# Moving three pieces of DVE work, and a group of transposes, in the output stage of a hybrid decoder layer

## The chip, the cores and the metric

The kernel runs on one core of a Trainium2 chip. The metric is the device time of one execution in microseconds (us). Several engines run their own instruction streams side by side and wait for each other by semaphores: TensorE (PE: matrix products and transposes), VectorE (DVE), ScalarE (ACT), GpSimd (POOL) and the DMA queues (SP issues most of them).

## What is computed

One layer of a decoder over 4096 prompt tokens and 64 sample tokens, model width 1024. The tokens are normalised and projected by `w_in`; three groups of heads (a gated convolution, sliding-window attention over 128 keys, and cross-attention into 256 memory tokens) give a row of 1024 values per token; `w_out` projects that back, and the result is normalised and added to the input.

```python
h = _rmsnorm(x, g_pre)
z = h @ w_in
cb, cc, ch, cg, q, k, v, ag, mq, mg = _split_cols(z)
...
out_a = jax.nn.silu(cg) * cb * conv                                  # convolution
out_b = jax.nn.silu(ag) * o_b        # o_b: window attention with sinks, 8 heads
out_c = jax.nn.silu(mg) * o_c        # o_c: attention into the memory tokens, 4 heads
y = jnp.concatenate([out_a, out_b, out_c], axis=-1) @ w_out
return x + _rmsnorm(y, g_post), new_conv, new_k, new_v
```

## The kernel before

**Stages.** The input projection comes first and lasts until about 918 us. Then attention and output projection run interleaved until the end. The prompt is cut into 16 chunks of 256 tokens; the two halves of a chunk have 128 tokens each and are numbered h = 0 to 31 (an even h is the first half of its chunk).

**Output projection.** The first six blocks of 128 tokens (blocks 0 to 5, `Block.run`) multiply `mix` (the 1024 values per token) with the eight 128-row slices of `w_out`, for each column half p and slice k. Every factor is split into a rounded part ("hi") and the remainder ("low"), so one slice is three products. From chunk 3 on two blocks are one `Pair` (c = 3 to 15, `Pair.run`): for the upper half of the inner dimension it uses Strassen-like sums, so that fewer products are needed. A pair has four accumulators, c12, c21, c11 and c22, and operands made ahead by POOL (the sum), ACT (the cast, "hi") and DVE (the subtraction, "low"): `pa` plain parts, `pr` row sums, `pw0` and `pw1` window parts, `pd` the diagonal sum, `pc` column differences. `lows` makes the two parts of any of them (L1676 the cast, L1679 the subtraction). `added` (L1755 for the second block) is the last addition of a pair: it reads the accumulator c22. L1772, L1775 and L1778 are the additions between c12, c21 and c11. L1761 and L1751 multiply with the norm's weights, L1740 squares and sums, L1746 copies an accumulator out.

**Finishing a block.** A finished block leaves a function in the list `left`: `finish` (L1658) multiplies by the norm's factor, adds the input `xr` in place and issues the store `o_yp<-xr`. `finish_block` empties that list.

**Attention.** For each half: window scores (`ws`, L1331), their masks and softmax on DVE and ACT (L1341, L1279, L1287, L1295 the division that gives `sm`), transposes of `sm_0` and `sm_1` on PE (`wt`, L1376), copies on ACT (`wpt`, L1305), selections on POOL that split the band (`wpv`, L1310, and `wpt`, L1313), and the products with the values (`wo`, L1388 and L1394). The cross-attention scores (`xs`) go through a maximum (L1169), exponentials on ACT (`xp`, L1178), a reciprocal (`xrd`, L1184), a scaling on POOL (L1190), transposes (`xt`, L1366), one ACT copy back to `xp` (L1367), and products (L1059).

**Order.** PE's order is written by hand in one manual schedule, until pair 13 begins; from there on it is left to the scheduler, up to the end of the last pair. The order counts in steps, "an eighth" in the words of the change: one step is one slice's three products. A block has 16 steps, a pair 30. `at(n, fn)` hangs a piece of work on step n; `first_at`, `memory_at` and `second_at` say at which step the scores, the cross-attention scores and the transposes of each half are issued. The other engines' orders follow a list scheduler, except for what `keep_in_program_order` pins. `between` is an existing list of work left for a later moment.

```python
turn_of = lambda odd, even: {h: start_of((h - 3) // 2) + (odd if h % 2 else even) for h in range(9, 2 * NCH + 1)}
second_at = {h: n + (12 if h == 2 else 9 if h == 8 else 8) for h, n in first_at.items()} | turn_of(18, 32)
...
at(e - 3, p.row_sums)
at(e + 4, lambda p=p: p.window_parts(0))
at(e + 7, lambda p=p: p.window_parts(1))
```

Here e is the first step of pair c, so `row_sums` of pair c is issued three steps before the end of pair c - 1.

**Weights of the pairs.** While blocks 0 to 5 run, the sums of `w_out` slices for the pairs (`wtT`, `wsumT`: L1842, L1847, L1848) are made on DVE and ACT, two of them are parked in memory, and they are loaded over slices of `wo` just before pair 3 (`wo<-tdT`).

Of the kernel before, what the change touches and what calls it, by code (L numbers as in the profile page):

```python
# [12 lines left out]
ALU = mybir.AluOpType  # L13
AX = mybir.AxisListType

P = 128
# [11 lines left out]
NCH = 4096 // CT  # L28
# [19 lines left out]
def f(ap):  # L48
    return ap.bitcast(F32)
# [3 lines left out]
def hybrid_layer(ctx: ExitStack, tc: tile.TileContext, a: dict):  # L53
# [1525 lines left out]
    class Block:  # L1579
# [38 lines left out]
        def run(self, starts):  # L1618
            b, m = self.b, self.m
            yn = work([P, D], "yn", f"yn{b}")  # L1620
            dst = a["o_ys"] if b == 32 else a["o_yp"][b * P : (b + 1) * P, :]
            st = tiny.tile([P, 4], F32, tag="ms", name=f"yst{b}")

            for p in range(2):
                cs = slice(512 * p, 512 * p + 512)
                acc = psum("z", f"y{b}_{p}")
                for k in range(KT):
                    starts.get((p, k), lambda: None)()
                    if m < P:
                        l, w = self.terms[p][k]  # L1630
                        for r in range(2):
                            TE.matmul(acc, l, w[:, r], start=k + r == 0, stop=k + r == KT)
                        continue
                    if (p, k) == (0, 5):
                        finish_block()
                    for i, (l, r) in enumerate(((0, 0), (1, 0), (0, 1))):
                        TE.matmul(acc, self.hl[l][:, k], wo[k][p][:, r], start=k + i == 0, stop=k + i == KT + 1)  # L1637
                if m < P:
                    S.copy(yn[:m, cs], acc[m : 2 * m])
                    V.tensor_tensor(yn[:m, cs], acc[:m], yn[:m, cs], op=ALU.add)  # L1640
                    junk = sums["sum"].tile([P, 512], F32, tag="sum", name=f"junk_s{p}")
                    S.activation(junk[:m], yn[:m, cs], AF.Square, scale=float(D) ** -0.5, accum_out=st[:m, p : p + 1])
                    V.tensor_tensor(yn[:m, cs], yn[:m, cs], gpost[:m, cs], op=ALU.mult)
                    continue
                V.tensor_tensor(yn[:m, cs], acc[:m], gpost[:m, cs], op=ALU.mult)
                S.activation(acc[:m], acc[:m], AF.Square, scale=float(D) ** -0.5, accum_out=st[:m, p : p + 1])  # L1646
            self.factor(st)
            left.append(lambda queued, part=None: self.finish(yn, st, dst, queued, part=part))
# [14 lines left out]
    class Pair:  # L1663
# [24 lines left out]
        def sums_of(self, raw, t, *terms):  # L1688
# [4 lines left out]
                G.tensor_tensor(raw[:, n * i : n * i + n], x, y, op=op)  # L1693
            return lambda pinned=False: self.lows(t, raw, pinned)

        def row_sums(self):
            t = self.parts("pr")
            self.rows = [t[:, :, 0:2], t[:, :, 2:4]]
            raw = sums["sum"].tile([P, 512], F32, tag="sum", name=f"sum{self.c}")
            self.sums_of(raw, t, *((self.mix(slice(2, 4), n), self.mix(slice(0, 2), n), ALU.add) for n in range(2)))()  # L1700

        def window_parts(self, n):
            t = self.w[n] = self.parts(f"pw{n}_")
# [17 lines left out]
        def run(self, starts, sample=lambda: None):  # L1721
            c, last = self.c, self.c == NCH - 1
# [30 lines left out]
            def added(n, p, acc):  # L1753
                cs = (left_, right_)[p]
                V.tensor_tensor(y[n][:, cs], acc, s3 if n else y[n][:, cs], op=ALU.add)  # L1755
# [36 lines left out]
            if not last:  # L1792
                c22 = psum("z", f"y{c}_c22")
                between.append(lambda: (scaled(0, 0, True), ends(0)))
                product(c22, self.down[0], t["T6"], True)
                product(c22, self.w[1], plain(1, range(4, 8)), False)
                added(1, 1, c22)
                scaled(1, 1)
                ends(1)
                return  # L1800
# [119 lines left out]
    first_at = {2: 4, 3: 20, 4: 34, 5: 48, 6: 62, 7: 76, 8: 89}  # L1920
    turn_of = lambda odd, even: {h: start_of((h - 3) // 2) + (odd if h % 2 else even) for h in range(9, 2 * NCH + 1)}
    memory_at = {h: n + (7 if h == 2 else 3 if h == 8 else 3) for h, n in first_at.items()} | turn_of(16, 27)
    second_at = {h: n + (12 if h == 2 else 9 if h == 8 else 8) for h, n in first_at.items()} | turn_of(18, 32)
    first_at |= turn_of(12, 24)

    what, pending = {}, []
    between = []

    def at(n, fn):
        what.setdefault(n, []).append(fn)  # L1930
# [17 lines left out]
    for c, p in pairs.items():  # L1948
        e = start_of(c)
        at(e - 10, p.plain_parts)  # L1950
        at(e - 3, p.row_sums)
        if c == NCH - 2:
            at(e + 27, lambda: left.pop(0)(True))
        at(e + 4, lambda p=p: p.window_parts(0))
        at(e + 5, lambda: pending.pop()() if pending else None)
        at(e + 6, lambda: left.pop(0)(True) if left else None)
        at(e + 7, lambda p=p: p.window_parts(1))
        at(e + (7 if c == NCH - 1 else 9), p.diagonal_sum)
        at(e + (8 if c == NCH - 1 else 11), p.column_differences)
        at(e + (9 if c == NCH - 1 else 11), lambda p=p: p.differences(True) if p.c == NCH - 1 else between.append(lambda: p.differences(True)))  # L1960
        at(start_of(c - 1) + 6, p.load)
        if c == NCH - 1:
            at(e + 4, finish_block)
# [146 lines left out]
```

## Time and profile before

| | us |
|---|---|
| median of 3 runs | 1528.67 (1528.08 to 1529.4) |
| profiled execution | 1541.16 |
| its span | 1539.4 |
| PE busy | 1510.8 |
| DVE busy | 1208.1 |
| ACT busy | 843.1 |
| POOL busy | 391.5 |

Busy times are of the one profiled execution. In the timelines a row is a group of like instructions that stand together: start, length, engine, line, operation, output<-inputs, count; in brackets the idle time of that engine just before, and what ended it. Lengths of matmuls that follow one another overlap a little, since their ends are modelled. Names are without their numbers: `pw` is `pw0` or `pw1`, `y_c` is any of the four accumulators of a pair, `place` is an alternate buffer of `mix`.

### The profile page before, as it was taken

What the parts mean: (1) busy time and instruction counts of PE and PEld (TensorE: products, weight loads), DVE (VectorE), ACT (ScalarE), POOL (GpSimd) and SP (SyncE); (2) the same over time, 40 slices, a digit from 0 to 9 for tenths busy, and PEclk for the clock granted to TensorE, in tenths of its full rate; (3) what the DMA queues carried; (4) which work ended last, traced back from release to release, by engine and by line L of the source; (5) the groups of instructions that cost most, each with busy time, mean ns of one, the idle gap of its engine ahead of it and who ended that gap; (6) DMA issues with size and microseconds to landing.
All of it is one profiled execution on the core that took longest, in us unless ns stands there. A gap on an engine that the chain in (4) does not pass through costs nothing.

```text
span 1539.4 us, 30947 instructions
## 1 busy us (share of the span) xinstructions
PE 1510.8 (98%) x11497; PEld 1386.8 (90%) x11497; DVE 1208.1 (78%) x2089; ACT 843.1 (55%) x2066; POOL 391.5 (25%) x576
## 2 busy tenths in 40 slices
PE   9999999999999999999999999999999999999997
PEld 9999999999999999999999999777788778777875
DVE  6779876899988777896777768876877888888864
ACT  6676655565422222354454536665666666666652
POOL 0222322211300000000111301234455444454631
PEclk9999999999999999999999999999999999999999
DMA  9989999878855333478787698998755555666552
GB/s 261 170 241 217 285 288 260 244 255 290 223 182 180 114 123 125 165 234 288 225 269 239 208 305 246 282 234 222 200 165 155 158 165 160 172 172 165 152 196 69
DMA packets 217322, 319.71 MB, mean 208 GB/s; under 512 B 37397, under 2 KB 143381, under 8 KB 217141
## 3 DMA queue, kind: packets, MB, share of 16 engines
q1 hardware_dynamic: 196837, 273.54, 60.5%
q0 software_dynamic: 19616, 43.15, 10.5%
q8 instruction: 91, 1.49, 0.4%
q10 hardware_dynamic: 720, 1.05, 0.2%
q14 instruction: 58, 0.48, 0.1%
HBM read 208.50 MB, written 110.15 MB: 207 GB/s over the span
## 4 chain that ended last, share of the span: by engine, by line
PE 68%; DVE 12%; issue 4%; DMA 4%; ACT 3%; POOL 1%; SPq 1%; DVEq 0%; ACTq 0%; POOLq 0%
PE c L368 49%; PE y_c L1737 9%; PE y L1637 2%; DVE sm L1295 2%; DVE sm L1341 1%; PE xt L1366 1%; DVE xr L1658 1%; DMA kst<-qd 1%; PE ws L1331 1%; DVE xmx L1169 1%; ACT sm L1287 1%; DMA nat<-in_x_p 1%; DVE wmx L1279 1%; PE mem_acc L790 1%; DMA zs<-in_w_out 1%
## 5 line engine op out<-in xcount | busy, mean ns | idle before, releaser
L375 DVE TENSOR_TENSOR z<-c,z 128x520 f32<-128x520 f32 (+1 forms) x308 | 194.3, 644 | 82.2 <-PE c L368 81.3
L1737 PE MATMUL y_c<-wo,pw 128*128 128x512 f32 (+1 forms) x636 | 158.4, 391 | 0.5 <-DVE yn L1775 0.5
L1287 ACT ACTIVATE sm<-sm,wnm 128x128 f32<-128x128 f32 x256 | 99.4, 389 | 72.0 <-DVE wnm L1281 72.0
L1737 PEld LDWEIGHTS y_c<-wo,pw 128*128 128x128 f32 x636 | 114.1, 188 | 27.2 <-issue 5.4
L1190 POOL TENSOR_SCALAR xp<-xp,xrd 128x256 f32<-128x256 f32 x128 | 67.6, 548 | 80.0 <-DVE xrd L1184 75.5
L1178 ACT ACTIVATE xp<-xs,xnm 128x256 f32<-128x256 f32 x128 | 59.0, 473 | 24.6 <-DVE xnm L1170 24.1
L737 POOL CAST wmask<-negs 128x256 uint8<-128x256 f32 x1 | 1.2, 1213 | 270.0 <-DMA negs<-in_wmask 270.0
L1313 POOL TENSOR_SCALAR_AFFINE_SELECT wpt<-wpt 128x512 f32<-128x512 f32 x64 | 59.0, 934 | 39.8 <-ACT wpt L1305 37.9
L1310 POOL TENSOR_SCALAR_AFFINE_SELECT wpv<-wpt 128x512 f32<-128x512 f32 x62 | 51.8, 848 | 58.5 <-ACT wpt L1305 58.4
L1637 PE MATMUL y<-wo,mh 128*128 128x512 f32 x192 | 64.5, 398 | 0.2 <-ACT y L1646 0.2
L276 ACT ACTIVATE nat<-nat 104x1024 f32<-104x1024 f32 x40 | 42.3, 1057 | 35.2 <-DMA nat<-in_x_p 35.2
L1331 PE MATMUL ws<-kst,q 128*128 128x256 f32 (+1 forms) x480 | 55.7, 297 | 0.0
L1341 DVE COPY_PREDICATED sm<-wmask,ws 128x512 f32<-128x512 uint8 x60 | 40.5, 729 | 18.5 <-ACT sm L1340 18.5
L1658 DVE SCALAR_TENSOR_TENSOR xr<-yn,yst,xr 128x1024 f32<-128x1024 f32 (+2 forms) x35 | 52.4, 1501 | 3.1 <-POOL yst L1653 3.0
L407 ACT CAST zh<-z 128x520 fp32r<-128x520 f32 x56 | 33.3, 624 | 36.5 <-DVE z L375 31.9
L377 ACT COPY z<-c 128x520 f32<-128x520 f32 (+1 forms) x44 | 24.4, 554 | 51.2 <-PE c L368 47.0
L1331 PEld LDWEIGHTS ws<-kst,q 128*128 128x128 f32 (+1 forms) x480 | 46.4, 187 | 4.1
L1287 ACT ACTIVATION_READ_ACCUMULATOR sm<-sm,wnm 128x1 f32 x256 | 47.9, 187 | 0.0
L1295 DVE TENSOR_TENSOR sm<-sm,wrd 128x512 f32<-128x512 f32 x64 | 44.8, 700 | 1.1
L164 POOL DMA_DIRECT2D md<-th x48 | 26.3, 548 | 75.6 <-DVE th L425 61.3
L1367 ACT COPY xp<-xt 128x1024 f32<-128x1024 f32 x30 | 30.4, 1014 | 27.1 <-POOL wpv L1310 16.1
L1737 PE MATMUL y_c<-wtT,pa 128*128 128x512 f32 x156 | 41.1, 400 | 3.8 <-DVE yn L1755 3.8
(1035 smaller groups left out, 5563.5 us busy)
## 6 DMA issues: line engine op xcount, KB each, us to landing
q<-qd SPq DMA_DIRECT2D x168, 128.0 KB
xr<-in_x_p SPq DMA_DIRECT2D x32, 512.0 KB
nat<-in_x_p SPq DMA_DIRECT2D x39, 416.0 KB
o_yp<-xr SPq DMA_DIRECT2D x31, 512.0 KB
kst<-qd SPq DMA_DIRECT2D x112, 128.0 KB
md<-th POOLq DMA_DIRECT2D x48, 260.0 KB, 7.3
qd<-zh SPq DMA_DIRECT2D x48, 260.0 KB
qd<-z SPq DMA_DIRECT2D x48, 260.0 KB
```

The source lines that it names most:

```text
L368: TE.matmul(bank[:, :HW], l, r, start=first and i == 0, stop=last and i == 3 * KH - 1)
L375: add = lambda dst, other: V.tensor_tensor(dst, c, other, op=ALU.add)
L1178: S.activation(p[:, i, :], s[:, i, :], AF.Exp, bias=nm[:, i : i + 1], scale=SCALE, accum_out=den[:, i : i + 1])
L1190: G.tensor_scalar(p[:, i, :], p[:, i, :], self.rds[h][:, i : i + 1], 0.5, op0=ALU.mult, op1=ALU.mult)
L1287: S.activation(sm[:, hh, :], sm[:, hh, :], AF.Exp, bias=nm[:, hh : hh + 1], scale=SCALE, accum_out=den[:, hh : hh + 1])
L1295: V.tensor_tensor(sm, sm, rd.unsqueeze(2).to_broadcast([P, 4, P]), op=ALU.mult)
L1313: G.affine_select(p3, p3, pattern=[[0, 4], [1, P]], compare_op=ALU.is_ge, fill=0.0, base=0, channel_multiplier=-1)
L1331: TE.matmul(out(kvh, col, bank), q(kvh, col, bank)[r], k(kvh, part)[r], start=first, stop=True, skip_group_check=not first, **place)
L1341: V.copy_predicated(sm4, third["wmask"].unsqueeze(1).to_broadcast([P, 2, 2, P]), s4[:, :, :, 0:P])
L1637: TE.matmul(acc, self.hl[l][:, k], wo[k][p][:, r], start=k + i == 0, stop=k + i == KT + 1)
L1658: x = V.scalar_tensor_tensor(self.xr[:m, cs], yn[:m, cs], st[:m, 3:4], self.xr[:m, cs], op0=ALU.mult, op1=ALU.add)
L1737: TE.matmul(acc, a[:, l, k], w[:, r, cs], start=first, stop=k == len(ws) - 1 and i == 2, skip_group_check=not new)
```

## The change

Four edits. First, `row_sums` for pairs 4 to 15 issues the cast as before, and hangs the subtraction (now a function of its own, `row_lows`) on a list `behind`, which `Pair.run` empties right after the last addition of the pair before. Second, the transposes of odd halves from 9 on go from step 18 to step 19. Third, block 5 no longer empties the list of finished blocks at its step (0, 5), so that block 4's residual is left to the next place where the list is emptied, the window probabilities of half 8. Fourth, in the last pair the second window parts are issued at step 5 instead of 7.

```diff
-                    if (p, k) == (0, 5):
+                    if (p, k) == (0, 5) and b < 2 * PLAIN_PAIRS - 1:
                         finish_block()
...
+        def row_lows(self, t, raw):
+            raw = raw.rearrange("p (b n) -> p b n", n=P)
+            tc.keep_in_program_order(V.tensor_tensor(t[:, 1], raw, f(t[:, 0]), op=ALU.subtract))
+
         def row_sums(self):
             t = self.parts("pr")
             self.rows = [t[:, :, 0:2], t[:, :, 2:4]]
             raw = sums["sum"].tile([P, 512], F32, tag="sum", name=f"sum{self.c}")
-            self.sums_of(raw, t, *((self.mix(slice(2, 4), n), self.mix(slice(0, 2), n), ALU.add) for n in range(2)))()
+            parts = self.sums_of(raw, t, *((self.mix(slice(2, 4), n), self.mix(slice(0, 2), n), ALU.add) for n in range(2)))
+            if self.c == PLAIN_PAIRS:
+                parts()
+            else:
+                S.copy(t[:, 0], raw.rearrange("p (b n) -> p b n", n=P))
+                behind.append(lambda: self.row_lows(t, raw))
...
                 added(1, 1, c22)
+                while behind:
+                    behind.pop(0)()
                 scaled(1, 1)
...
-    second_at = {h: n + (12 if h == 2 else 9 if h == 8 else 8) for h, n in first_at.items()} | turn_of(18, 32)
+    second_at = {h: n + (12 if h == 2 else 9 if h == 8 else 8) for h, n in first_at.items()} | turn_of(19, 32)
...
-    between = []
+    between, behind = [], []
...
-        at(e + 7, lambda p=p: p.window_parts(1))
+        at(e + (5 if c == NCH - 1 else 7), lambda p=p: p.window_parts(1))
```

The changed kernel's line numbers from L1696 on are higher by 9, and from L1808 on by 11, so L1755 becomes L1764, L1761 L1770, L1775 L1784 and L1737 L1746.

DVE where pair 6 follows pair 5, before (`yn5_1` is the last addition of pair 5, `pr6` the low part of pair 6's row sums, `sm14_1` the second softmax of half 14):

```order
L1295 TENSOR_TENSOR sm14_1_14799<-sm14_1_14799,wrd14_1_14835 128x512
L1679 TENSOR_TENSOR pr6_14881<-sum6_14882,pr6_14881 128x512
L1184 RECIPROCAL xrd7_0_14873<-xden7_0_14867 128x2
L1755 TENSOR_TENSOR yn5_1_14440<-y5_c22_14746,s3_5_14443 128x512
L1184 RECIPROCAL xrd7_1_14877<-xden7_1_14870 128x2
```

and now:

```order
L1295 TENSOR_TENSOR sm14_1_14799<-sm14_1_14799,wrd14_1_14835 128x512
L1764 TENSOR_TENSOR yn5_1_14440<-y5_c22_14746,s3_5_14443 128x512
L1184 RECIPROCAL xrd7_0_14873<-xden7_0_14867 128x2
L1698 TENSOR_TENSOR pr6_14881<-sum6_14882,pr6_14881 128x512
L1184 RECIPROCAL xrd7_1_14877<-xden7_1_14870 128x2
```

The addition and the subtraction have changed places around the first reciprocal.

POOL in pair 6, from its row sum on, before:

```order
L1693 TENSOR_TENSOR sum6_14882<-place_159 128x256
L1693 TENSOR_TENSOR diag6_14993<-place_159 128x256
L1190 TENSOR_SCALAR xp7_0_14866<-xp7_0_14866,xrd7_0_14873 128x256 x2
L1190 TENSOR_SCALAR xp7_0_14866<-xp7_0_14866,xrd7_1_14877 128x256 x2
```

and now:

```order
L1693 TENSOR_TENSOR sum6_14882<-place_159 128x256
L1190 TENSOR_SCALAR xp7_0_14866<-xp7_0_14866,xrd7_0_14873 128x256 x2
L1693 TENSOR_TENSOR diag6_14993<-place_159 128x256
L1190 TENSOR_SCALAR xp7_0_14866<-xp7_0_14866,xrd7_1_14877 128x256 x2
```

`diag6` shares its buffers with the row sums, so it comes behind the subtraction that reads them, and the first two scalings of the memory attention go ahead of it.

POOL a little further on, at the odd half 15, before:

```order
L1310 AFFINE_SELECT wpv15_0_15162<-wpt15_0_15160 128x512
L1313 AFFINE_SELECT wpt15_0_15160<-wpt15_0_15160 128x512
L1190 TENSOR_SCALAR xp7_1_15129<-xp7_1_15129,xrd7_2_15136 128x256 x2
L1190 TENSOR_SCALAR xp7_1_15129<-xp7_1_15129,xrd7_3_15140 128x256 x2
L1310 AFFINE_SELECT wpv15_1_15167<-wpt15_1_15165 128x512
L1313 AFFINE_SELECT wpt15_1_15165<-wpt15_1_15165 128x512
```

and now:

```order
L1190 TENSOR_SCALAR xp7_1_15129<-xp7_1_15129,xrd7_2_15136 128x256 x2
L1190 TENSOR_SCALAR xp7_1_15129<-xp7_1_15129,xrd7_3_15140 128x256 x2
L1310 AFFINE_SELECT wpv15_0_15165<-wpt15_0_15163 128x512
L1310 AFFINE_SELECT wpv15_1_15170<-wpt15_1_15168 128x512
L1313 AFFINE_SELECT wpt15_0_15163<-wpt15_0_15163 128x512
L1313 AFFINE_SELECT wpt15_1_15168<-wpt15_1_15168 128x512
```

All four selections now stand behind the four scalings. ACT's order follows it: both copies `wpt` now stand behind the exponentials `xp`, and on PE one step of three products with `pc` has gone ahead of the transposes.

DVE in block 5, before (`xr4` is block 4's residual; it stands between the two operations named `wsumT11` and `wtT11`):

```order
L1652 TENSOR_SCALAR yst4_13021<-yst4_13021 128x1
L1842 TENSOR_TENSOR wsumT11_13078<-wsumT11_13078,zs_12003 128x512
L1658 SCALAR_TENSOR_TENSOR xr4_12455<-yn4_13020,yst4_13021,xr4_12455 128x1024
L1848 TENSOR_TENSOR wtT11_13300<-wsumT11_13078,wtT11_13300 128x512
L1645 TENSOR_TENSOR yn5_13288<-y5_0_13290,gpost_11647 128x512
```

and where it is now, in the softmax of half 8:

```order
L1283 TENSOR_TENSOR wes8_1_13432<-wnm8_1_13430,sink_8466 128x4
L1658 SCALAR_TENSOR_TENSOR xr4_12455<-yn4_13020,yst4_13021,xr4_12455 128x1024
L1292 TENSOR_TENSOR wden8_0_13423<-wden8_0_13423,wes8_0_13420 128x4
L1294 RECIPROCAL wrd8_0_13443<-wden8_0_13423 128x4
L1295 TENSOR_TENSOR sm8_0_13410<-sm8_0_13410,wrd8_0_13443 128x512
```

The residual has gone past `wtT11`, block 5's first `yn5` and the score masks of half 8. On SP's queue its store moves from between the loads `wo_0<-tdT` to between the loads `wo_1<-tdT`.

PE's order in the last pair, before, goes from the twelve products with `pw0_15` to the sample scores (`sms`), four products with `pd15`, six with `pw1_15`, two with `pd15` and two with `pw1_15`; now three products with `pw1_15` stand ahead of `sms`, three behind them, and then the six with `pd15` without a break.

## Prediction

> **What bounds the kernel now.** I read the page's totals first, then the list of what TensorE (PE) waits for from 1050 us to the end, then the timeline around each wait the change touches.
>
> ```profile
> span 1539.4 us, 30947 instructions
> PE 1510.8 (98%) x11497; PEld 1386.8 (90%) x11497; DVE 1208.1 (78%) x2089; ACT 843.1 (55%) x2066; POOL 391.5 (25%) x576
> ```
> ```profile
> PE y_c L1737 <- DVE yn L1755: 3.8, 11, 0.6
> PE wt L1376 <- DVE sm L1295: 1.8, 10, 0.4
> PE y_c L1737 <- ACT yn L1746: 0.8, 1, 0.8
> ```
>
> PE is busy for 98% of the span, so a faster DVE, ACT or POOL is worth only the PE idle time that it ends. The list (total us, times, longest) gives the places: the first product of a new pair waits 11 times for the last addition of the old one, the odd half's second group of transposes waits 10 times for the softmax division, and the last pair waits once for an ACT copy. It names no DMA. A fourth place lies ahead of that window, in block 5.
>
> **Part A, block 4's residual leaves block 5.** PE here, and the same section in pair 6 for comparison (the window's row gives the granted clock):
>
> ```profile
> 1043.52 1.03 PE L1366 MATMUL xt<-ident,xp 128*128 128x128 f32 x8
> 1044.31 1.86 PE L1331 MATMUL ws<-kst,q 128*128 128x256 f32 x16
> 1047.84 0.60 PE L1388 MATMUL wo<-wpv,vt 64*64 64x256 f32 x2 [1.67 <-ACT xp L1367]
> 1051.95 0.50 PE L1637 MATMUL y<-wo,mh 128*128 128x512 f32 x1
> ...
> 1193.52 0.43 PE L1388 MATMUL wo<-wpv,vt 64*64 64x256 f32 x2
> ...
> 1196.00 0.50 PE L1737 MATMUL y_c<-wo,pc 128*128 128x512 f32 x1
> ```
> ```profile
> 1048.00:1050.00 2.00, 2.00 (x14) 0.83 (x11) 1.78 (x3) 0.67 (x2) 0.00 (x0) 0.50 0.93 346
> ```
>
> PE stands still for 1.67 us, and then the clock is 0.50: the section from wo to the next product takes 1051.95 - 1047.84 = 4.11 us against 1196.00 - 1193.52 = 2.48 us, so 1.63 us more. Stall and half clock cost 3.30 us together. What the copy waited for:
>
> ```profile
> 1042.79 1.64 DVE L1658 SCALAR_TENSOR_TENSOR xr<-yn,yst,xr 128x1024 f32<-128x1024 f32 x1 [0.90 <-POOL yst L1653]
> 1044.36 1.12 DVE L1848 TENSOR_TENSOR wtT<-wsumT,wtT 128x512 fp32r<-128x512 f32 x1
> 1045.39 0.68 DVE L1645 TENSOR_TENSOR yn<-y,gpost 128x512 f32<-128x512 f32 x1
> ```
> ```profile
> 1041.92 0.62 ACT L1847 CAST wtT<-wsumT 128x512 fp32r<-128x512 f32 x1 [0.25 <-DVE wsumT L1842]
> 1046.10 0.58 ACT L1646 ACTIVATE y<-y 128x512 f32<-128x512 f32 x1 [3.56 <-DVE yn L1645]
> 1046.69 1.00 ACT L1367 COPY xp<-xt 128x1024 f32<-128x1024 f32 x1
> ```
> ```profile
> 1044.88 1.67 POOL L1313 TENSOR_SCALAR_AFFINE_SELECT wpt<-wpt 128x512 f32<-128x512 f32 x2
> ```
>
> The removed row is the head of a chain: residual, wtT, yn, ACT's square, ACT's copy, PE. Without it wtT starts when its cast ends, 1041.92 + 0.62 = 1042.54, and ends by 1043.7 even at 1.12 us. yn then ends by 1044.4, the square by 1045.0, and the copy, whose input PE transposed by 1043.52 + 1.03 = 1044.55, by 1046.0. PE's scores end at 1044.31 + 1.86 = 1046.17, so nothing waits. The nearest other producer is POOL's wpt, done at 1046.55 beside a busy DVE; I put it at about 1045.6 once that DVE work is gone (estimate, two selects at 0.64 us as in the row of 1192.08 below). If it doesn't move, 0.4 us of stall stays.
>
> The residual comes back in half 8, between wes_1 and wden_0, ahead of the division that releases wt. It costs DVE 1.64 us there; the next PE wait in that stretch is this one:
>
> ```profile
> 1065.08 2.99 PE L1737 MATMUL y_c<-wo,pw 128*128 128x512 f32 x12 [0.46 <-DVE yn L1775]
> ```
>
> I let it grow by 0.3 us (bounds 0 and 1.64, the whole instruction; DVE has idle stretches between, so near the low end). On SP's queue the store moves behind three weight loads, and the loads of kst, vT and q for the next half queue behind it. No DMA ends a PE wait in the list, so I cost that at nothing. If the cover goes, the first score product of the next pair waits for kst. Part A: -3.30 + 0.30 = **-3.0 us** (bounds -3.3 and -1.3, below).
>
> The Trainium skill, page "TensorE: Matmul & The Clock Gate", Part 1, has PE fall to half rate after an idle window of about 3.4 us. The trace shows 0.50 after only 1.67 us. If that page's figure held, the half clock would have another cause and would stay, and the sum would lose 1.63 us: 1525.0 instead of 1523.4, still within the likeliest case's own range.
>
> **Part B, the last pair's window parts come earlier.**
>
> ```profile
> 1501.20 0.57 ACT L1746 COPY yn<-y_c 128x512 f32<-128x512 f32 x1
> 1501.83 1.55 PE L1737 MATMUL y_c<-wtT,pd 128*128 128x512 f32 x4 [0.83 <-ACT yn L1746]
> ```
>
> PE waits 0.83 us, until the copy ends at 1501.77, with the diagonal products next in its order. The new order puts window products there that need neither the copy nor a late cast: three before the sample scores and three behind. Six at about 0.23 us (12 take 2.9 us in the rows of pair 6) are 1.4 us of work to put into the wait. The gain is at least 0.83 and at most 1.4 us; I take **-1.2**, since the row behind it (the diagonal products broken off after four) was fed late too.
>
> **Part C, the pairs.** The even half, pair 6:
>
> ```profile
> 1167.64 0.38 PE L1912 MATMUL vtp<-ident,vT 128*128 128x128 f32 x2
> 1168.35 1.65 PE L1737 MATMUL y_c<-wtT,pa 128*128 128x512 f32 x6 [0.33 <-DVE yn L1755]
> ...
> 1172.56 2.92 PE L1737 MATMUL y_c<-wo,pw 128*128 128x512 f32 x12
> ...
> 1204.15 1.66 PE L1737 MATMUL y_c<-wtT,pa 128*128 128x512 f32 x6 [0.32 <-DVE yn L1755]
> ```
> ```profile
> 1166.95 0.68 DVE L1679 TENSOR_TENSOR pr<-sum,pr 128x512 fp32r<-128x512 f32 x1
> ...
> 1167.62 0.67 DVE L1755 TENSOR_TENSOR yn<-y_c,s 128x512 f32<-128x512 f32 x1
> ...
> 1171.66 0.68 DVE L1775 TENSOR_TENSOR yn<-s,y_c 128x512 f32<-128x512 f32 x1
> ```
> ```profile
> 1167.71 0.73 POOL L1693 TENSOR_TENSOR diag<-place 128x256 f32<-128x256 f32 x1 [4.85 <-DVE xrd L1184]
> 1168.42 2.29 POOL L1190 TENSOR_SCALAR xp<-xp,xrd 128x256 f32<-128x256 f32 x4
> ```
>
> The same product of the next pair starts at 1204.15, so a pair takes 35.80 us. The two 0.68 us operations change places, so the addition ends at 1167.62 instead of 1168.29. The wait removed is 0.35 us by the list (3.8 / 11) and up to 0.71 - 0.19 = 0.52 us by starts (two transposes at about 0.1). But DVE's L1775 doesn't move: ACT's casts and pw's low part stand before it. It ends at 1172.34 and PE needs it at 1172.56, so only 0.22 us can be kept. Against that, pr's low part now runs beside POOL's first xp, and diag waits for it.
>
> What such a meeting costs, a few us on (DVE's product reads two SBUF tiles):
>
> ```profile
> 1190.62 0.89 DVE L1751 TENSOR_TENSOR yn<-yn,gpost 128x512 f32<-128x512 f32 x1 [0.93 <-ACT s L1740]
> ```
> ```profile
> 1189.13 1.85 POOL L1190 TENSOR_SCALAR xp<-xp,xrd 128x256 f32<-128x256 f32 x4
> 1190.93 1.08 POOL L1310 TENSOR_SCALAR_AFFINE_SELECT wpv<-wpt 128x512 f32<-128x512 f32 x1
> 1192.08 0.64 POOL L1313 TENSOR_SCALAR_AFFINE_SELECT wpt<-wpt 128x512 f32<-128x512 f32 x1
> ```
>
> DVE takes 0.89 instead of 0.68 us, POOL 1.08 instead of 0.64: 0.2 and 0.44 us. So POOL's xp end about 0.4 us later and meet pw's low part, which can lose 0.2 us. The even half keeps between +0.22 and about 0; I take 0.
>
> The Trainium skill, page "SBUF — State Buffer", section "Who interferes with whom", says that a DVE instruction with two SBUF inputs and a GpSimd instruction that reads SBUF exclude each other for a whole instruction. The rows fit. What a full exclusion would do is the fifth rival below.
>
> The odd half:
>
> ```profile
> 1186.34 0.63 PE L1376 MATMUL wt<-ident,sm 128*128 128x128 f32 x4 [0.16 <-DVE sm L1295]
> 1186.72 1.63 PE L1737 MATMUL y_c<-wo,pc 128*128 128x512 f32 x6
> ```
> ```profile
> 1187.56 0.47 ACT L1178 ACTIVATE xp<-xs,xnm 128x256 f32<-128x256 f32 x1
> ```
> ```profile
> 1474.87 1.85 POOL L1190 TENSOR_SCALAR xp<-xp,xrd 128x256 f32<-128x256 f32 x4 [4.56 <-PE wt L1376]
> ...
> 1478.31 1.22 POOL L1313 TENSOR_SCALAR_AFFINE_SELECT wpt<-wpt 128x512 f32<-128x512 f32 x2
> ```
>
> Three products (0.7 us) now lie ahead of the transposes, so their wait goes: 0.18 us by the list, 0.28 as I take it. The price is on POOL: before, wpv_0 and wpt_0 ran at 1187.66, ahead of xp; now all four selects follow xp. Pair 14 has this order already: from the first xp to the end of wpt_1 it takes 1478.31 + 1.22 - 1474.87 = 4.66 us. With xp released by ACT's second pair of exponentials at about 1188.7, wpt_1 ends near 1193.4, against 1192.72 before, and PE wants it at 1193.52 - 0.28 = 1193.24. A new wait of some 0.2 us eats most of the 0.28. Net 0.1 us per pair; times 11 pairs, **-1.1 us** (bounds: all waits gone, (0.43 + 0.28) x 11 = -7.8; or the wait on POOL of the fourth rival).
>
> **Sum.** -3.0 - 1.2 - 1.1 = -5.3 us. The profiled execution took 1541.16 us, 12.5 above the median of the runs, so it would become 1535.9; the median 1528.67 becomes 1523.4. A measurement of this kernel can tell about 0.2% (3.06 us) from no change.
>
> **Rivals.** First: the pairs lose nothing in place of their stalls, because DVE's later work moves up as well. -3.0 - 1.2 - 7.8 = -12.0, 1516.7. For it speaks that the list names no POOL wait in the pairs; against it L1775's margin of 0.22.
>
> Second: block 5 stays as it is, since another wait takes the residual's place there. -1.2 - 1.1 = -2.3, 1526.4. For it: POOL's wpt ended at 1046.55, 0.4 us behind PE's need; against: it ran beside the very operations that leave.
>
> Third: the pairs get 0.3 us longer each, by pw's low part (0.2) in the even half and a little more wait at wo in the odd. -4.2 + 3.3 = -0.9, 1527.8.
>
> Fourth, slower: POOL's selects become the bound of the odd half. If each of the four takes 1.08 us, as the one beside DVE did, wpt_1 ends at 1188.7 + 1.85 + 4.32 = 1194.9, PE waits 1.6 us at wo and loses 1.4 net, eleven times: -4.2 + 15.4 = +11.2, 1539.9. It decides from 0.66 us per pair on ((4.2 + 3.06) / 11), that is with wpt_1 later than about 1194.2. Pair 14's four selects took 2.8 us, not 4.3, which speaks against it.
>
> Fifth, slower too: pr's low part and POOL's xp exclude each other for the whole 0.68 us, and all of it reaches PE in every even half by way of POOL's later selects and pw's low part: -4.2 + 7.5 = +3.3, 1532.0. Against it: the meeting shown above cost 0.2 and 0.44 us, and pair 6's selects have no PE wait behind them.
>
> **Chances.** Forecast 0.56; first rival 0.12; second 0.10; third 0.14; fourth 0.06; fifth 0.02. Faster by over 0.2% are the forecast and the first, 0.68; within 0.2% the second and third, 0.24; slower 0.08. The range 1516.5 to 1528.5 takes in the first three rivals and leaves out the fourth and fifth and what lies beyond the first. The likeliest case alone: 1520.5 to 1525.5.
>
> **What would show it.** Block 5: no PE wait on ACT's xp ahead of wo, and the clock at 1.00 there. Tail: no wait on L1746. Pairs: the row for the addition (now L1764) gone from the list of PE waits, a row for the subtraction after it (L1784) or for POOL's wpt at wo in its place, the period of a pair within 0.3 us of the 35.8 before. I am wrong if that period moves by more, or if wo in block 5 waits for POOL.

## The result, and the profile after

Over 21 runs each, taken in turn, the changed kernel takes 1524.87 us in the median (before 1530.39); the ratio is 0.9962, with a 95% interval of 0.995 to 0.9973. That is 5.8 us less (4.1 to 7.7) where 5.3 were forecast. A second series gave 0.996 (0.9943 to 0.9978).

The page of the changed kernel, and the list of what PE waits for from 1040 us on:

```profile
span 1527.0 us, 30947 instructions
PE 1507.6 (99%) x11497; PEld 1384.4 (91%) x11497; DVE 1199.3 (79%) x2089; ACT 843.5 (55%) x2066; POOL 398.5 (26%) x576
```
```profile
PE y_c L1746 <- DVE yn L1784: 0.6, 1, 0.6
PE wt L1376 <- DVE sm L1295: 0.4, 1, 0.4
PE y_c L1746 <- ACT y L1646: 0.2, 1, 0.2
PE y L1632 <- DVE mh_s L1605: 0.2, 1, 0.2
```

The list's eleven waits for the last addition (now L1764) are gone, ten waits for L1295 have become one, and the copy L1755 in the last pair isn't waited for any more. The two spans differ by 12.4 us, but 4.6 us of that lie before chunk 3's vT transposes (1022.31 us before, 1017.72 now), where no code has changed: that is how far single executions lie apart. So everything below is read between fixed places behind that point.

**Block 5.** PE, the granted clock, and the producers:

```profile
1039.71 1.86 PE L1331 MATMUL ws<-kst,q 128*128 128x256 f32 x16
1041.51 0.43 PE L1388 MATMUL wo<-wpv,vt 64*64 64x256 f32 x2
...
1043.99 0.50 PE L1637 MATMUL y<-wo,mh 128*128 128x512 f32 x1
```
```profile
1041.50:1043.50 2.00, 2.00 (x28) 1.32 (x28) 1.50 (x3) 0.96 (x2) 0.13 (x1) 1.00 1.00 370
```
```profile
1040.05 1.01 ACT L1367 COPY xp<-xt 128x1024 f32<-128x1024 f32 x1
```
```profile
1039.71 1.22 POOL L1313 TENSOR_SCALAR_AFFINE_SELECT wpt<-wpt 128x512 f32<-128x512 f32 x2
```

The copy ends at 1041.06 and POOL's wpt at 1040.93, both before PE has finished its scores at 1041.57; nothing waits, and the section takes 1043.99 - 1041.51 = 2.48 us at full clock. POOL's selects became shorter with the DVE work gone (1.22 us for two, 1.67 before), as estimated.

**The even half of pair 6.**

```profile
1159.70 0.38 PE L1923 MATMUL vtp<-ident,vT 128*128 128x128 f32 x2
1159.84 1.63 PE L1746 MATMUL y_c<-wtT,pa 128*128 128x512 f32 x6
...
1164.07 2.99 PE L1746 MATMUL y_c<-wo,pw 128*128 128x512 f32 x12
```
```profile
1158.54 0.68 DVE L1764 TENSOR_TENSOR yn<-y_c,s 128x512 f32<-128x512 f32 x1
...
1160.77 1.17 DVE L1770 TENSOR_TENSOR yn<-yn,gpost 128x512 f32<-128x512 f32 x1
...
1163.22 0.68 DVE L1784 TENSOR_TENSOR yn<-s,y_c 128x512 f32<-128x512 f32 x1
```

From the vT transposes to the next product it is 0.14 us instead of 0.71, so the wait is gone, and no new one stands at the pw0 products: L1784 starts 3.52 us behind the vT transposes, where it had been 4.02. DVE meets POOL as expected, but that reaches nobody: the product L1770 takes 1.17 us, 0.68 before, and POOL's first two scalings take 1.29 where four took 1.85 undisturbed.

```profile
1159.39 1.29 POOL L1190 TENSOR_SCALAR xp<-xp,xrd 128x256 f32<-128x256 f32 x2 [4.95 <-DVE xrd L1184]
```

**The odd half.** The row to look at is the last of the first fence:

```profile
1184.71 0.43 PE L1388 MATMUL wo<-wpv,vt 64*64 64x256 f32 x2
1184.73 0.43 PE L1388 MATMUL wo<-wpt,vt 64*64 64x256 f32 x1
1184.98 0.38 PE L1388 MATMUL wo<-wpv,vt 64*64 64x256 f32 x2
1184.99 0.93 PE L1388 MATMUL wo<-wpt,vt 64*64 64x256 f32 x3
```
```profile
1180.58 1.85 POOL L1190 TENSOR_SCALAR xp<-xp,xrd 128x256 f32<-128x256 f32 x4 [5.82 <-DVE xrd L1184]
...
1184.01 1.22 POOL L1313 TENSOR_SCALAR_AFFINE_SELECT wpt<-wpt 128x512 f32<-128x512 f32 x2
```

Before, the eight small products L1388 came in four pairs close together (the last row 0.38 us long); now two of those with wpt come late, since wpt_1 ends only at 1184.01 + 1.22 = 1185.23. From the first wo product to L1059 it takes 2.06 us (1.51 before). This wait of 0.55 us is in no list: the stall lies inside a group of small products whose times in the profile overlap, so PE never counts as idle. It is seen in a row's length alone.

**The tail.** The first three of the second window products (`pw1`) are now part of the row ahead of the sample scores (fifteen products, twelve before), and three more stand behind them:

```profile
1485.78 3.70 PE L1746 MATMUL y_c<-wo,pw 128*128 128x512 f32 x15
1489.41 1.09 PE L1463 MATMUL sms<-skm,smp 128*32 128x256 f32 x16
1490.43 0.98 PE L1746 MATMUL y_c<-wo,pw 128*128 128x512 f32 x3
```

All profiles of this study, by PE's starts, in us. "Block 5" is from chunk 3's vT transposes to chunk 4's, "pair 3" from there to chunk 5's, "pair" the mean of the next eight, "tail" from chunk 15's to PE's last product.

| kernel | block 5 | pair 3 | pair | tail |
|---|---|---|---|---|
| before | 37.81 | 35.91 | 35.80 | 75.03 |
| before, again | 36.11 | 35.97 | 35.82 | 74.98 |
| changed | 34.39 | 36.64 | 35.49 | 73.24 |
| changed, again | 34.35 | 36.57 | 35.46 | 73.20 |
| first edit alone | 36.11 | 35.98 | 35.81 | 74.98 |
| second edit alone | 36.13 | 36.07 | 35.45 | 74.44 |
| third edit alone | 34.35 | 36.47 | 35.82 | 75.00 |
| fourth edit alone | 37.76 | 35.90 | 35.82 | 73.41 |
| without the first edit | 34.33 | 36.55 | 35.46 | 72.91 |
| the same, again | 34.30 | 36.57 | 35.46 | 72.86 |
| split transposes | 34.35 | 36.39 | 35.70 | 73.44 |
| split, copy first | 34.35 | 36.37 | 35.70 | 73.42 |
| PE held back | 36.09 | 37.17 | 36.48 | 75.46 |
| no residual of block 4 | 34.36 | 36.20 | 35.49 | 73.27 |

### The profile page after: what moved, and what is told of

It reads as the page before. It is cut to its first block, busy times and chain, and to the rows that moved or that the text cites. A ratio compares the mean times of both kernels' runs of the same rounds, so it can differ in the third digit from the quotient of the medians.

```text
span 1527.0 us, 30947 instructions
## 1 busy us (share of the span) xinstructions
PE 1507.6 (99%) x11497; PEld 1384.4 (91%) x11497; DVE 1199.3 (79%) x2089; ACT 843.5 (55%) x2066; POOL 398.5 (26%) x576
## 3 DMA queue, kind: packets, MB, share of 16 engines
q8 instruction: 91, 1.49, 0.4%
## 4 chain that ended last, share of the span: by engine, by line
PE 75%; DMA 11%; DVE 6%; issue 4%; POOL 2%; ACT 1%; SPq 1%; DVEq 0%; ACTq 0%; POOLq 0%
PE c L368 39%; PE y_c L1746 16%; PE y L1637 3%; PE ws L1331 3%; DMA nat<-in_x_p 2%; DMA md<-th 2%; PE wo L1394 2%; PE wo L1059 2%; PE xs L1353 2%; PE xt L1366 2%; PE wt L1376 2%; PE wo L1388 2%; DMA place<-in_xt 1%; DMA wr_3A<-in_w_in 1%; DMA hd_B<-place 1%
## 5 line engine op out<-in xcount | busy, mean ns | idle before, releaser
L1746 PE MATMUL y_c<-wo,pw 128*128 128x512 f32 (+1 forms) x636 | 158.9, 392 | 0.6 <-DVE yn L1784 0.6
L1746 PEld LDWEIGHTS y_c<-wo,pw 128*128 128x128 f32 x636 | 114.0, 188 | 27.8 <-issue 5.4
L1190 POOL TENSOR_SCALAR xp<-xp,xrd 128x256 f32<-128x256 f32 x128 | 71.8, 577 | 196.9 <-DVE xrd L1184 192.3
L1310 POOL TENSOR_SCALAR_AFFINE_SELECT wpv<-wpt 128x512 f32<-128x512 f32 x62 | 56.9, 939 | 8.7 <-ACT wpt L1305 8.4
L1313 POOL TENSOR_SCALAR_AFFINE_SELECT wpt<-wpt 128x512 f32<-128x512 f32 x64 | 46.3, 742 | 38.6 <-ACT wpt L1305 38.2
L1295 DVE TENSOR_TENSOR sm<-sm,wrd 128x512 f32<-128x512 f32 x64 | 44.5, 696 | 1.1
L1746 PE MATMUL y_c<-wo,pc 128*128 128x512 f32 (+1 forms) x162 | 45.2, 400 | 0.0
L1637 PEld LDWEIGHTS y<-wo,mh 128*128 128x128 f32 x192 | 36.1, 188 | 8.9 <-issue 1.0
```

What stands on the lines that cost most here:

```text
L1190: G.tensor_scalar(p[:, i, :], p[:, i, :], self.rds[h][:, i : i + 1], 0.5, op0=ALU.mult, op1=ALU.mult)
L1295: V.tensor_tensor(sm, sm, rd.unsqueeze(2).to_broadcast([P, 4, P]), op=ALU.mult)
L1310: G.affine_select(pv.rearrange("p (h q) -> p h q", h=4), p3, pattern=[[0, 4], [-1, P]], compare_op=ALU.is_gt, fill=0.0, base=0, channel_mu ...
L1313: G.affine_select(p3, p3, pattern=[[0, 4], [1, P]], compare_op=ALU.is_ge, fill=0.0, base=0, channel_multiplier=-1)
L1746: TE.matmul(acc, a[:, l, k], w[:, r, cs], start=first, stop=k == len(ws) - 1 and i == 2, skip_group_check=not new)
```

## The experiments

**Each edit alone.** The four edits of the change, one at a time on the kernel before; their diffs are those of the change. Theory A: the waits in a pair share one slack, that of DVE and ACT against PE. Its rival B: each wait is worth what it shows.

> The first edit alone: pr's low part behind the last addition of the pair before. In the changed kernel the pair takes 35.49 us (35.80 before), the waits on DVE (0.57 at the addition, 0.35 at the odd half's transposes, by PE's starts) are gone and a new one of 0.55 us stands inside the odd half's wo products. Theory A (the waits share one slack: DVE and ACT follow PE's scores, so a PE wait at wo gives them a lead that the even half then uses; without it L1775 binds): the addition's wait goes, a wait of 0.3 to 0.5 us at the first pw0 product takes its place, period 35.55 to 35.75, whole kernel -1 to -3 us. Theory B (the waits are independent): the even half keeps all 0.57, period 35.2 to 35.3, whole kernel -5.5 to -6.5 us.

Measured: ratio 0.9996 (0.9976 to 1.0016), period 35.81. The addition's wait is gone and the same time stands elsewhere:

```profile
1158.22 1.64 PE L1746 MATMUL y_c<-wtT,pa 128*128 128x512 f32 x6
1159.99 3.10 PE L1746 MATMUL y_c<-wo,pr 128*128 128x512 f32 x12
```
```profile
1158.73 0.64 ACT L1749 ACTIVATE s<-yn 128x512 f32<-128x512 f32 x1
...
1159.34 0.59 ACT L1779 COPY s<-y_c 128x512 f32<-128x512 f32 x1
```

PE's row sums must wait until ACT has copied c12 out (1159.93), and ACT does that behind its exponentials and a square; the products before take 1.77 us by starts instead of 1.49. Another 0.21 us is lost between the start of the row sums and that of the window products (2.93 us instead of 2.72), and the rest in small pieces. B has fallen. A had the mechanism right, that the wait goes elsewhere; its place is ACT's copy and not DVE's subtraction, and its size is the whole wait, so that the period stays above A's 35.55 to 35.75.

> The second edit alone: transposes of odd halves one step later. Theory A: the new wait of about 0.5 us at wo appears and gives DVE the lead, so that the addition's wait shrinks from 0.57 to about 0.1 although nothing was done to it; period 35.45 to 35.6, about the same as with both edits; whole kernel -2.5 to -4 us. Theory B: the addition's wait stays at 0.57, 0.35 is won and 0.55 lost, period 35.95 to 36.05, whole kernel +1.5 to +3 us.

Measured: ratio 0.9951 (0.9933 to 0.9968), period 35.45. Its first fence is the start of pair 6, the second the odd half's wo:

```profile
1158.49 0.38 PE L1912 MATMUL vtp<-ident,vT 128*128 128x128 f32 x2
1158.70 1.65 PE L1737 MATMUL y_c<-wtT,pa 128*128 128x512 f32 x6
```
```profile
1183.81 0.86 PE L1388 MATMUL wo<-wpt,vt 64*64 64x256 f32 x3
```

The wait inside wo is there (1.99 us for the section, so 0.48), and the addition's wait, to which nothing was done, went from 0.57 to about 0.07 (0.21 by starts instead of 0.71). That is A, and the period lies in A's range. The runs of this kernel, fewer than of the others, say 5 to 10 us, more than A's 2.5 to 4; its profile accounts for 4, of which 0.55 us is the tail (74.44 against 75.0).

> The third edit alone: block 5 leaves block 4's residual to half 8. If the residual heads the chain that PE waits for, the wait on ACT's xp ahead of wo is gone, the section from wo to the next product takes 2.48 us and the clock is 1.00 there; from the transposes of vT of chunk 3 to those of chunk 4 (37.81 us before) it is 34.4; the pairs' period stays 35.80; whole kernel -2.5 to -3.2 us. If POOL's wpt was the real bound, 0.4 us or more of the wait stays and with it perhaps the half clock: -0.5 to -1.5 us.

Measured: ratio 0.9981 (0.9968 to 0.9994), 2.9 us; block 5 in 34.35 us, no wait and full clock, the pair unchanged. The residual did head the chain. But pair 3 takes 36.47 instead of 35.9.

> The fourth edit alone: the last pair's second window parts two steps earlier. The wait of PE on ACT's L1746 in the last pair (0.83 us in the list, 1.2 by starts, and 0.34 behind it) goes; from the last vT transposes to PE's last matmul 1.2 to 1.8 us less than the 75.03 before; nothing changes ahead of it. Whole kernel -1 to -2 us.

Measured: the tail is 73.41 us, 1.6 less, as expected; the wait for L1746 is gone. In the runs that can't be told (ratio 1.0003, 0.9989 to 1.0016).

**Is the first edit worth anything beside the second?** The changed kernel with the old `row_sums`:

```diff
-            parts = self.sums_of(raw, t, *((self.mix(slice(2, 4), n), ...
-            if self.c == PLAIN_PAIRS:
-                parts()
-            else:
-                S.copy(t[:, 0], raw.rearrange("p (b n) -> p b n", n=P))
-                behind.append(lambda: self.row_lows(t, raw))
+            self.sums_of(raw, t, *((self.mix(slice(2, 4), n), ...))()
```

> The changed kernel without its first edit (pr's low part where it was). With the second edit alone the pair took 35.40 to 35.51 us, with all four 35.49, and the first edit alone left it at 35.81. Theory A (one shared slack): the first edit adds nothing on top of the second, so period 35.40 to 35.50, the block 5 stretch at 34.4 and the tail as in the changed kernel, the whole kernel within 2 us of the changed one, ratio to before 0.993 to 0.998. Theory B (the first edit is worth 0.3 us a pair or more): period 35.75 or longer, 3 us or more slower than the changed kernel.

> The changed kernel without the first edit, beside the changed one on the same chip. Theory A gives 0.04 us per pair and so half a microsecond less than the changed kernel; a difference of more than 2 us either way would need something outside the pairs.

> The changed kernel once more, on the chip of the next one: period 35.49, 0.994 to 0.998 of before.

Measured: 0.9955 (0.9939 to 0.9971) in the first series; in the second, on one chip with the changed kernel, 0.994 (0.9919 to 0.996) against 0.996 (0.9943 to 0.9978). The period is 35.46 in both its profiles, 35.49 and 35.46 in those of the changed kernel. The first edit adds nothing to the pairs. In the second series the medians with and without it are 1523.58 and 1520.97 us, 2.6 apart and so more than the 2 allowed, but the intervals overlap; the profiles show a loss of 0.3 to 0.35 us in the tail with it and no other difference that large, so the rest stays unexplained.

**Can the new wait be had back?** Two variants of the changed kernel. In the first, the odd half's first group of transposes goes back to step 18, and only the second group stays at 19:

```diff
-            chunks[c].window_turns(i)
+            chunks[c].window_turns(i, (1,) if i and h >= 9 else (0, 1))
...
+    for h, n in second_at.items():
+        if h % 2 and h >= 9 and h // 2 < NCH:
+            at(n - 1, lambda h=h: chunks[h // 2].window_turns(1, (0,)))
```

> The changed kernel, with the odd half's first group of transposes back at step 18 and only the second at step 19. ACT's first copy and POOL's first pair of selects then stand ahead of xp again, so that wpt_1 is done some 0.9 us earlier and the 0.55 us inside wo go. Theory A: with that the lead of DVE and ACT goes too, and the wait of the first edit alone comes back, PE's row-sum products behind ACT's copy of c12 (0.3 us by starts there, up to 0.4): period 35.3 to 35.5. Theory B: nothing takes the place of the 0.55, period 34.95 to 35.05, another 6 us faster than the changed kernel.

Measured: 0.9972 (0.9952 to 0.9992), period 35.70, 0.2 more than the changed kernel and more than A allowed. The wait inside wo is gone (1.51 us), and two stand in its place:

```profile
1153.06 1.63 PE L1748 MATMUL y_c<-wtT,pa 128*128 128x512 f32 x6
1154.83 3.10 PE L1748 MATMUL y_c<-wo,pr 128*128 128x512 f32 x12
...
1171.16 0.94 PE L1748 MATMUL y_c<-wo,pc 128*128 128x512 f32 x3
1172.13 0.66 PE L1378 MATMUL wt<-ident,sm 128*128 128x128 f32 x4
```

The row sums start 1.77 us behind the products before them, as with the first edit alone (ACT's copy of c12), and the second transposes start 0.97 us behind the three products ahead of them, which take 0.69 in the changed kernel (1177.15 to 1177.84); the event that releases them is ACT's copy of the first group. In the second variant that copy of c12 goes ahead of the square as well:

```diff
             S.copy(s3, c12)
+            while later:
+                later.pop(0)()
...
-                scaled(1, 1)
-                ends(1)
+                later.append(lambda: (scaled(1, 1), ends(1)))
```

> As the split kernel, and ACT's copy of c12 is issued ahead of the square of the pair before (0.82 us with its read-out), which in the first edit alone stood in front of it while PE waited. If ACT's order at the pair's start is what binds once wo doesn't, the row-sum products wait for nothing and the period falls to 35.0 to 35.2; the whole kernel 4 to 6 us below the changed one. If DVE's chain (pw's low part, then the subtraction from c12) binds right behind it, the wait moves to the first pw0 product and the period stays at 35.3 to 35.5.

Measured: 0.9969 (0.9953 to 0.9984), period 35.70 again. The row sums' first half waits no more, and the second half does:

```profile
1154.61 1.54 PE L1748 MATMUL y_c<-wo,pr 128*128 128x512 f32 x6
1156.36 1.65 PE L1748 MATMUL y_c<-wo,pr 128*128 128x512 f32 x6 [0.21 <-DVE s L1785]
```

DVE's addition of c21 writes the buffer that the square uses, and the square now comes later. The waits move from one operation of that chain to the next and the period stays.

**A lead made by hand.** The kernel before, with PE held back at the place where the second edit holds it back:

```diff
+            if i == 1 and self.c >= 4:
+                for n in range(5):
+                    TE.transpose(banks[:, 0, :P], ident, ident)
```

> The kernel before, with five useless transposes of the identity (0.1 us each) on PE ahead of the odd half's wo products, from half 9 on; all else as before. PE has 0.5 us more work per pair. Theory A (DVE and ACT get a lead where PE is held back behind the scores, and the lead ends other waits): the wait at the last addition (0.57 by starts) shrinks by about as much as was put in, and the period stays at 35.75 to 35.9; whole kernel within 1.5 us of before. Theory B (waits are independent): period 36.3, whole kernel +5.5 to +6.5 us.

Measured: 1.006 (1.004 to 1.008), period 36.48. Both numbers are nearer to B, but B's ground isn't there: the addition's wait did go in full (0.14 us from the vT transposes to the next product, as without a wait; 0.71 before). What made up for it is a new wait of 0.52 us, at the cross-attention scores:

```profile
1153.35 0.84 PE L1740 MATMUL y_c<-wo,pw 128*128 128x512 f32 x3
1154.54 1.18 PE L1353 MATMUL xs<-mk,q 128*128 128x256 f32 x8 [0.35 <-issue]
```
```profile
1152.22 1.28 DVE L1661 SCALAR_TENSOR_TENSOR xr<-yn,yst,xr 128x1024 f32<-128x1024 f32 x1
1153.42 0.68 DVE L1253 TENSOR_TENSOR place<-place,wo 128x512 f32<-128x512 f32 x1
1154.02 0.41 DVE L1408 TENSOR_TENSOR place<-place,wo 128x256 f32<-128x256 f32 x1
```

The scores start 0.1 us after DVE has read the last of wo, and DVE had put a residual of 1.28 us ahead of that reading: the scores take over wo's buffers, and with the added transposes the scheduler chose another order on DVE. The five transposes themselves took 0.70 us, not 0.5. So 0.70 went in, 0.57 was saved and 0.52 came on top, which is the 0.68 us that the pair grew by, within 0.03. The experiment shows that the lead ends the addition's wait; as a test of the period it is spoilt. Without the new wait the period would have been about 36.0 (an estimate from these three numbers).

**What pair 3 lost.** The changed kernel without block 4's residual:

```diff
+            if b == 8:
+                left.pop(0)
             finish_block(True)
```

> The changed kernel with block 4's residual and its store left out altogether (block 4's part of the output isn't written). In the changed kernel the stretch from chunk 4's vT transposes to chunk 5's takes 36.64 us against 35.9 to 36.0 before: PE waits there for ACT's square of block 5 and for DVE's subtraction L1784. If the residual's return to half 8 is what costs that, the stretch falls to 35.9 to 36.1 here; if PE only arrives earlier at work that comes when it comes, it stays at 36.4 to 36.7. The stretch before it stays at 34.4 in both cases.

Measured: pair 3 takes 36.20 us, between the two theories. In the changed kernel two waits stand there, and only one is left:

```profile
1052.66 1.65 PE L1746 MATMUL y_c<-wtT,pa 128*128 128x512 f32 x6 [0.17 <-ACT y L1646]
...
1057.61 3.00 PE L1746 MATMUL y_c<-wo,pw 128*128 128x512 f32 x12 [0.58 <-DVE yn L1784]
```
```profile
1048.45 3.01 PE L1748 MATMUL y_c<-wo,pw 128*128 128x512 f32 x12 [0.59 <-DVE yn L1786]
```

So some 0.4 us of the 0.65 lost is the residual, by way of ACT's square (from chunk 4's vT transposes to the next product it is 0.14 us without the residual and 0.55 with it), and the rest isn't.

**The half clock.** The kernel before once more:

> The kernel before, profiled once more, for the half clock behind block 5's stall. The stall of 1.7 us stands in four profiles so far (before, and the first, second and fourth edit alone); two of them show the clock at 0.50 behind it (37.8 us for that stretch) and two show 1.00 (36.1 us). If the half clock comes by chance with the phase of something, this profile shows one of the two values and the stall of 1.7 us in either case; if the half clock belongs to the program, it shows 37.8 us.

Measured: the same stall, at full clock behind it:

```profile
1035.28 0.43 PE L1388 MATMUL wo<-wpv,vt 64*64 64x256 f32 x2 [1.69 <-ACT xp L1367]
...
1037.76 0.50 PE L1637 MATMUL y<-wo,mh 128*128 128x512 f32 x1
```

Six profiles have this stall (before, before again, the first, second and fourth edit alone, and PE held back). In two of them the clock fell to one half (37.8 us for block 5), in four it didn't (36.1 us).

The recorded clock tells the two apart. In each of the 14 profiles the granted clock changes only at points that lie a whole number of stretches of 3.41 us from each other, and the half clock behind the stall lasts exactly one such stretch. In the kernel before, the whole stall lies inside one stretch, and the next has the half clock (the first number behind the length is PE's busy time; the clock is the third from the end):

```profile
1044.57:1047.98 3.41, 1.75 (x20) 1.43 (x23) 1.50 (x2) 1.88 (x4) 2.67 (x4) 1.00 1.00 315
1047.98:1051.39 3.41, 3.41 (x24) 1.90 (x23) 2.76 (x7) 1.27 (x6) 0.00 (x0) 0.50 0.99 356
```

In the kernel before once more, a border cuts the same stall into 1.13 and 0.56 us:

```profile
1031.31:1034.73 3.42, 2.28 (x23) 1.94 (x20) 2.20 (x3) 1.18 (x3) 3.37 (x4) 1.00 0.99 293
1034.73:1038.14 3.41, 2.86 (x34) 2.00 (x35) 2.48 (x5) 1.38 (x3) 0.00 (x0) 1.00 0.96 311
```

All six profiles go this way: with the fourth edit alone the stall is uncut too, and in the three others it is cut, with no more than 1.20 us in one stretch. So the half clock depends on where the stall falls in these stretches, which differs from execution to execution.

## Why the prediction was right

The sum was right and its parts were not: one was too large and two too small. That the errors nearly cancel is luck. By the profiles part A gave 1.1 or 2.7 us instead of 3.0, B up to 1.8 instead of 1.2 and C 3.4 instead of 1.1; together 6.3 us where the clock holds and 7.9 where it falls, against 5.8 (4.1 to 7.7) in the runs.

**Part A, -3.0 us.** The chain was read rightly: without the residual nothing waits at wo, POOL's wpt included, and the second rival is out. The step that failed is the 1.63 us of half clock. It was taken from one execution as if it belonged to the program; four of six executions with the same stall don't have it. The other reading that the forecast allowed for, that the half clock has another cause and stays, isn't borne out: none of the eight profiles without the stall shows it in block 5. Without the half clock, block 5 gains 36.1 - 34.4 = 1.7 us. The term for the residual's return, 0.3 us, was too small: pair 3 lost 0.6 to 0.7, of which the run without the residual puts 0.4 on it. Together 1.1 us where the clock holds and 2.7 where it falls. The lower bound of 1.3 didn't allow for the first.

**Part B, -1.2 us.** Right in mechanism, and 1.6 in size by the fourth edit alone. The bound of 1.4 counted the products put into the wait; the broken-off diagonal group's second stall went too. The changed kernel's tail is 1.8 us shorter, but that holds 0.55 us which the second edit gives by itself and some 0.35 which the first takes.

**Part C, -1.1 us.** From chunk 5's vT transposes to chunk 15's it is 355.13 us against 358.51, so -3.4. The odd half's new wait on wpt_1 came where it was forecast, at 0.55 us instead of 0.2: pair 14's 4.66 us from xp to the end of wpt_1 held (1185.23 - 1180.58 = 4.65), but xp started 0.3 us later behind the exponentials than assumed. The step that failed is that this wait was taken off the gain at the transposes. It costs nothing, since it takes the place of the even half's wait for the addition.

The reason is where DVE and ACT get their input. They take up the next softmax from PE's scores, which come before wo, and they don't wait for PE inside wo. The odd half's scores ahead of pair 6, before, in the changed kernel, and with the second edit alone (with its last addition):

```profile
1155.92 1.86 PE L1331 MATMUL ws<-kst,q 128*128 128x256 f32 x16
```
```profile
1147.43 1.86 PE L1331 MATMUL ws<-kst,q 128*128 128x256 f32 x16
```
```profile
1146.27 1.86 PE L1331 MATMUL ws<-kst,q 128*128 128x256 f32 x16
```
```profile
1157.97 0.67 DVE L1755 TENSOR_TENSOR yn<-y_c,s 128x512 f32<-128x512 f32 x1
```

The addition ends 12.37 us behind the start of these scores before (1168.29 - 1155.92), and 12.37 with the second edit alone (1158.64 - 1146.27), though PE stood still in wo in between. The next pair's first product starts 12.43 us behind the scores in both. Before, PE got there early and waited; now it has spent that time inside wo. The table cuts a pair at two places of PE's order (by starts; means of seven pairs, in us), and gives the ends of two DVE operations behind the start of the scores:

| kernel | even half's L1059 to odd half's scores | these scores to the next pair's pw0 products | end of the last addition | end of the operation that is L1775 before |
|---|---|---|---|---|
| before | 12.31 | 16.64 | 12.38 | 16.42 |
| first edit alone | 12.36 | 16.56 | 11.72 | 16.40 |
| second edit alone | 11.95 | 16.66 | 12.39 | 16.44 |
| changed | 11.95 | 16.67 | 11.80 | 16.48 |
| split transposes | 12.23 | 16.56 | 11.71 | 16.40 |
| split, copy first | 12.24 | 16.58 | 11.71 | 16.39 |
| PE held back | 12.32 | 17.32 | 12.32 | 17.10 |

The rest of a pair takes 6.84 to 6.90 us in all of them. In the second column the waits for the addition, inside wo, for ACT's copy of c12 and for DVE's addition of c21 stand in for each other, and it hardly moves except in the kernel held back. What the change gains is the first column, 0.36 us: the odd half's transposes wait no more, and they lie ahead of the scores. The split kernels keep most of that wait, and that is what they lose. "L1775 doesn't move" was right, measured from the scores: it ends 16.42 us behind them before and 16.48 now, 0.16 to 0.22 us ahead of the pw0 products in every kernel of the table. It is 0.50 us earlier against the vT transposes only because PE reaches those 0.57 us later behind the scores. So the 0 us of the even half was right, and the 0.28 us of the odd half should have stayed whole. That the new wait fits into the slack, 0.55 us against 0.57, is luck too: the forecast had it at 0.2. By starts the sum per pair is -0.57 (addition) -0.35 (transposes) +0.55 (wo) and 0.06 spread over the rest: -0.31.

My view of the first edit as a part of the gain was wrong: alone it moves the addition's wait to the row sums, and beside the second it adds nothing. That DVE and ACT don't follow PE through wo is shown by the third column: with the addition in its old place it ends 12.38 us behind the scores without a wait in wo and 12.39 with it, and with the first edit 11.72 and 11.80. PE held back has the 0.52 us at the cross-attention scores in its second column on top.

**The rivals.** The first (the pairs keep 0.71) failed by half: all the old stalls did go, and 0.55 came back. The third (pairs 0.3 us longer) fell, since they became 0.31 shorter. The fourth had the right place, POOL's selects at wo; they took 2.85 us, like pair 14's, not 4.3. On the fifth: DVE and POOL did hold each other up (L1770 by 0.49 us, two xp by 0.36), and none of it reached PE. The Trainium skill, page "SBUF — State Buffer", section "Who interferes with whom", has a DVE instruction with two SBUF inputs contend with a GpSimd instruction that reads SBUF, which agrees with those lengths; here they cost PE nothing. What I named as a sign of error, a period off by more than 0.3 us, just came about.

## What to carry to other kernels

When PE is 98% busy and waits in several places of a loop for the same engines, don't add the waits up: find the point where the others take their input. Waits between that point and the place where PE needs their result share one slack, so that ending one lets another grow; a wait ahead of that point counts in full. Try each edit alone, and measure the stretches between such points and not the waits. A group of small overlapping products can hide a stall from every list of waits, so compare the length of the same section in two profiles. And before a slower clock seen in one profile goes into a sum, look whether a second execution has it, and where the stall ahead of it lies between the points at which the clock can change.

## What the runs showed of the hardware that was not expected

The same idle time of 1.7 us on PE was followed by a granted clock of one half in two profiles of six, and by full clock in four, with the same instructions around it. What decided it is how much of the idle time fell into one of the stretches of 3.41 us between which the clock can change. Counted over all such stretches of the 14 profiles from 40 us to the clock's last change (PE's idle time by the profile, whose ends of matmuls are modelled), each of the sixteen with 1.69 us or more was followed by half clock: fourteen at the kernels' ends, one in the input projection of the kernel before (from 266.33 us, 2.31 us idle) and one in block 5 with the fourth edit alone. None with 1.26 us or less was. Between these lie two, one of 1.67 us with half clock behind it (block 5 before) and one of 1.68 us without (the end of the fourth edit's profile). So the limit in these profiles lies at about half a stretch.

The Trainium skill, page "TensorE: Matmul & The Clock Gate", Part 1, speaks of an idle window of about 3.4 us that runs freely, so that its effect varies from run to run. The length and the variation agree; but the window needn't be idle throughout, since half of it was enough twice here.
